# Attention queries and keys loaded straight into TensorE's operand tiles, without staging and casts, with some assumed delays longer

## The chip, the cores and the metric

The kernel runs on one core of one Trainium2 chip. The metric is the device time of one execution, in microseconds (us). The numbers below come from three timed runs and from one profiled execution of the kernel before.

## The reference

One transformer block over 1024 tokens with a model width of 1024, all in float32. A normalised input `h` is projected to four mixers and to 4 x 1024 gates; the mixers' outputs are multiplied by the gates, added, projected by `w_out`, and a convolutional feed-forward part follows.

```
proj = rms_norm(x, g) @ w_in            # s5, sgu, deltanet, attention q k v, 4 x 1024 gates
merged = sum(sigmoid(gate_b) * (mixer_b(...) @ w_br[b]) for b in range(4))
x = x + merged @ w_out
x = x + conv_ffn(rms_norm(x), ...);  return rms_norm(x)

# the attention mixer (diff_attention): 4 heads, each with two maps of 32 channels
s = q . k / sqrt(32) - slope[h] * (qpos - kpos), causal
p = softmax(s);  pd = p[map 0] - lam * p[map 1]
o = rms_norm(pd @ v) * (1 - lam_init)
```

## The kernel before

Matrix products are made to float32 accuracy from float32r operands: a tile is split into a rounded high part (`hi`) and the rest (`lo`), and each product is three matmuls (hi hi, lo hi, hi lo). The kernel's work after the first normalisation is in these stages: the mixers (deltanet, s5, attention projections, sgu), the attention itself (`diff`), the gates that are left, the merge of the four branches, `w_out`, and the feed-forward part.

**The order of the work** is written by `weave` (line 110). It holds a few generators, the *tasks*, and one more, the *filler* (`gates`: 30 blocks of gate columns, 48 matmuls of 512 columns each). A task that has issued what it can yields a number: the delay in us that its author assumes until its next matmuls will have their inputs, most of them from the table `LAT` (line 1733). `weave` counts the matmul time that it has emitted (`pe.now`), and a task whose delay has not passed yet is left alone: another task is taken, and if none is ready a piece of filler. A delay that is too short puts a matmul on TensorE's in-order queue before its inputs are there, and TensorE stands; a longer one puts more of the other tasks' matmuls or of filler in between. What is left of the filler when the tasks are done is run at once, before the merge. Each engine takes its instructions in the order in which they were placed on it.

There are two weaves that matter. In the first, one task is the deltanet (`dn_pair` for two pairs of heads) and then `diff_begin`, which prepares the attention; the other is `z_in`, `s5`, `diff_in` and `sgu`. In the second, the only task is `diff`.

**The attention's operands.** `diff_in` (line 865) projects queries, keys and values of two blocks of 128 channels (`b` = 0, 1: heads 0 and 1, heads 2 and 3) and stores them to DRAM from SP's queue: for each of q and k a tensor of three stacked parts (q: hi, hi, lo; k: hi, lo, hi), so that one matmul over 96 rows makes all three products. `diff_begin` (line 901) computes a few constants, turns the values to tokens (`diff_v`, line 988: a load of 512 KB from SP's queue into a staging tile `stg`, a delay `LAT["dv"]`, transposes on TensorE) and calls `diff_prep`. `diff_prep` (line 958) makes eight operand tiles `stkq0..3`, `stkk0..3` of 105 rows x 1024: it loads 96 rows of q or k and 9 rows of position terms ("alibi") into one of three `stg` tiles, with two DMAs from GpSimd's queue (POOL in the profile), and ScalarE (ACT) casts the staging tile to the operand tile in float32r (line 969). `diff` (line 929) runs the heads 0 to 3; after head 0 it calls `diff_prep` for `b` = 1, whose tiles take the same space as those of `b` = 0, so a cast waits until the head that used that tile is done. `diff_norm` also uses two `stg` tiles.

**Other places the change touches.** `dn_pair` puts 6 transposes on TensorE, yields `LAT["row"]` and then issues a matmul on `rowl` (line 612), which VectorE (DVE) makes at line 609. `s5_groups` (8 times) transposes two tables, yields 0 at line 1212 and then issues a matmul on `NA` (line 1216), a table that DVE finishes at line 1195. After the last group `s5` yields `LAT["s5z"]` (line 1298), loads `z` back from DRAM, splits it into `zh` and `zl` and multiplies.

POOL also makes the `lo` parts of the filler's weights (`glo`, line 152) and of q and k (`ql`), and one product of sgu (`ws`, line 808), which needs the load `tri`.

Of the kernel before, what the change touches and what calls it, by code (L numbers as in the profile page):

```python
# [11 lines left out]
F32 = mybir.dt.float32  # L12
F32R = mybir.dt.float32r
# [8 lines left out]
P = 128  # L22
L = 1024
# [72 lines left out]
class Builder:  # L96
# [438 lines left out]
    def dn_pair(self, pool, pr, src):  # L535

        nc = self.nc
        v = nc.vector
        sq, sk, sv = src
# [46 lines left out]
        rows = []  # L586
# [17 lines left out]
        wq = self.t(pool, [P, 8, 256], F32, "WQ")  # L604
        kq = self.t(pool, [P, 8, 2, 128], F32, "KQ")
        gl = self.t(pool, [P, 16], F32, "gl")
        yield LAT["row"]
        r = self.t(pool, [32, 8, 2], F32R, "rowl")
        v.tensor_tensor(r, pt2[0:32, 128:256].rearrange("p (c t) -> p c t", t=64)[:, :, 63].unsqueeze(1).to_broadcast([32, 8, 2]),
                        delta.unsqueeze(2).to_broadcast([32, 8, 2]), op=ALU.mult)  # L610
# [114 lines left out]
        for ch in range(16):  # L725
            yield LAT["state"] if ch else LAT["wT"]
            m, hf = ch // 2, ch % 2
            rows, other = slice(64 * hf, 64 * hf + 64), slice(64 - 64 * hf, 128 - 64 * hf)
            u = rk_tile[rows, m, 0].rearrange("p h d -> p (h d)")
            p1 = self.ps()  # L730
# [4 lines left out]
            p2 = self.ps()  # L735
# [25 lines left out]
        y = self.t(pool, [P, L], F32, "row", 2)  # L761
        for f in range(2):
            s = slice(512 * f, 512 * f + 512)
# [101 lines left out]
    def diff_in(self):  # L865

        nc = self.nc
        self.qkdram = {}
        self.vdram = []
        with ExitStack() as st:  # L870
            pool = self.pool(st, "dqk", side="right")
            for w, blk in (("q", B_DQ), ("k", B_DK), ("v", B_DV), ("v", B_DV + 1), ("q", B_DQ + 1), ("k", B_DK + 1)):
                b = blk % 2
                if w == "v":
                    d = self.t(self.dp, [P, L], F32, f"dv{b}")
                    self.vdram.append(d)
                else:
                    d = self.t(self.dp, [3, P, L], F32, f"dq{w}{b}")
                    self.qkdram[w, b] = d

                f = self.t(pool, [P, L], F32, "qf", 1)
                if w != "v":
                    hi, lo = self.t(pool, [P, L], F32R, "qh", 1), self.t(pool, [P, L], F32R, "ql", 1)

                def evac(s, ps):
                    if w == "q":
                        nc.scalar.activation(f[:, s], ps, AF.Copy, scale=32.0 ** -0.5)
                    else:
                        nc.scalar.copy(f[:, s], ps)
                    if w != "v":  # L890
                        self.split(hi[:, s], lo[:, s], f[:, s], nc.scalar, nc.gpsimd)

                yield from self.project(blk, evac)
                if w == "v":
                    nc.sync.dma_start(d, f)
                    continue
                for i, x in enumerate((hi, hi, lo) if w == "q" else (hi, lo, hi)):
                    nc.sync.dma_start(d[i], x.bitcast(F32))
        self.projected = True

    def diff_begin(self, stack):

        nc, v = self.nc, self.nc.vector
        while not self.projected:
            yield 1.0
        pool = self.operands = self.pool(stack, "operands", side="left")

        lq = self.t(pool, [P, 2, 2, 32], F32, "lq")
        nc.sync.dma_start(lq, self.a["diff_l"])
        lp = self.t(pool, [P, 2, 32], F32, "lp")  # L910
        ls = self.t(pool, [P, 2], F32, "ls")
        v.tensor_tensor(lp, lq[:, 0], lq[:, 1], op=ALU.mult)
        v.tensor_reduce(ls, lp, axis=AX.X, op=ALU.add)
        le = self.exp_small(pool, ls, [P, 2], "le")
        nlam = self.t(pool, [P, 1], F32, "nlam")
        v.tensor_tensor(nlam, le[:, 1:2], le[:, 0:1], op=ALU.subtract)
        v.tensor_scalar(nlam, nlam, -LAM_INIT, None, op0=ALU.add)
        idb = self.t(pool, [P, 128], BF16, "idb")
        cmb = self.t(pool, [P, 128], BF16, "cmb")
        v.tensor_copy(idb, self.ident)  # L920
        v.tensor_copy(cmb, self.c[:, C_CAUSAL:C_CAUSAL + 128])
        self.diff_consts = nlam, idb, cmb

        self.vhl = self.t(pool, [P, 8, 4, 128], F32R, "vhl")
        for x in range(2):
            yield from self.diff_v(pool, self.vhl, x)
        self.stk = [self.diff_prep(pool, 0)]

    def diff(self, pool):
        nc = self.nc  # L930
        v = nc.vector
        stk, vh = self.stk, self.vhl
        nlam, idb, cmb = self.diff_consts

        held = None
        for h in range(4):
            b, hl = divmod(h, 2)
            for i in range(8):
                if h or i:
                    yield max(0.0, free - self.pe.now)  # L940
                p0 = self.diff_scores(pool, i, stk[b], hl, nlam, idb, cmb)
                done = self.pe.now + LAT["p"] + LAT["p1"] * (i + 1)
                if held:
                    yield max(0.0, held[-1] - self.pe.now)
                    yield from self.diff_values(pool, vh, *held[:-1])
                if i == 0 and hl == 0:
                    if b:
                        yield from self.diff_norm(pool, 0, ob)
                    ob = self.t(pool, [P, L], F32, "ob", 1)
                free = self.pe.now if i < 3 else done - LAT["p2"]  # L950
                held = h, i, p0, ob, done
            if h == 0:
                stk.append(self.diff_prep(self.operands, 1))
        yield max(0.0, held[-1] - self.pe.now)
        yield from self.diff_values(pool, vh, *held[:-1])
        yield from self.diff_norm(pool, 1, ob)

    def diff_prep(self, pool, b):

        nc = self.nc  # L960
        v = nc.vector
        stk = {}
        for hl, w in itertools.product(range(2), "qk"):
            for hm in range(2 * hl, 2 * hl + 2):
                s = self.t(pool, [105, L], F32R, f"stk{w}{hm}", 1)
                g = self.t(pool, [P, L], F32, "stg", 3)[0:105]
                nc.gpsimd.dma_start(g[0:96, :], self.qkdram[w, b][:, 32 * hm:32 * hm + 32, :])
                nc.gpsimd.dma_start(g[96:105, :], self.a["alibi_q"][2 * b + hm // 2] if w == "q" else self.a["alibi_k"])
                nc.scalar.copy(s, g)
                stk[w, hm] = s  # L970
        return stk

    def diff_norm(self, pool, b, ob):
        nc = self.nc
        v = nc.vector
        y = self.t(self.operands, [P, L], F32, "stg", 3)
        sq = self.t(self.operands, [P, L], F32, "stg", 3)
        nc.scalar.activation(sq, ob, AF.Square)
        yield LAT["sq"]
        r = self.rms_scale(pool, sq, self.c[:, C_BLK64:C_BLK64 + 128:64], 1.0 / 64)  # L980
        yield LAT["rsqrt"]
        for f, r in enumerate(self.rms_rows(r, 2)):
            s = slice(512 * f, 512 * f + 512)
            v.tensor_tensor(y[:, s], ob[:, s], r, op=ALU.mult)
            v.tensor_scalar(y[:, s], y[:, s], self.col("diff_norm_g"), 1.0 - LAM_INIT, op0=ALU.mult, op1=ALU.mult)
        nc.sync.dma_start(self.ydram[3][:, b, :], y)

    def diff_v(self, pool, vh, b):

        vf = self.t(pool, [P, L], F32, "stg", 3)  # L990
        self.nc.sync.dma_start(vf, self.vdram[b])
        yield LAT["dv"]
        for f in range(2):
            pt = self.to_tokens(vf, f).rearrange("p (m h d) -> p m h d", m=4, h=2)
            sl = slice(4 * f, 4 * f + 4)
            hi = vh[:, sl, 2 * b:2 * b + 2, 0:64]
            self.nc.scalar.copy(hi, pt)
            self.nc.vector.tensor_tensor(vh[:, sl, 2 * b:2 * b + 2, 64:128], pt, hi.bitcast(F32), op=ALU.subtract)
# [176 lines left out]
    def s5_groups(self, pool, g0, NG, udram, zdram):  # L1175
        nc = self.nc
        v, g_ = nc.vector, nc.gpsimd
        p = self.s5p
# [26 lines left out]
        for W, tag, sc in ((W1, "sF", 1.0), (W2, "sG", -1.0)):  # L1205
# [3 lines left out]
            x = self.t(pool, [P, NG, 128], F32, tag)  # L1209
            nc.scalar.mul(x.rearrange("p g c -> p (g c)"), pt[:, 0:128 * NG], sc)  # L1210
            wt.append(x)
        yield 0.0

        pk = self.ps()
        for g in range(NG):
# [32 lines left out]
        for x, tab, dst in ((wt[0], CT, z), (wt[1], ST, z2)):  # L1248
            pv = self.ps()
# [4 lines left out]
        f = "p g c -> p (g c)"  # L1254
# [12 lines left out]
        y = self.t(pool, [P, NG, 128], F32, "zin")  # L1267
# [462 lines left out]


W_BUFS = {"w": 3, "g": 4, "raw": 2}
LAT = {'dng': 14.76, 'tok': 2.33, 'tok2': 0.31, 'rows': 11.3, 'row': 1.76, 'decay': 0.47, 'gram': 2.75, 'gram2': 0.05, 'subst': 40.0, 'inverse': 10.0, 'solve': 2.1, 'wT': 1.2, 'state': 0.72, 'u': 1.17, 'out': 10.15, 'gelu': 0.93, 'vt': 0.8, 'mix': 0.52, 's5p': 49.2, 's5': 4.25, 's5z': 6.6, 's5v': 1.98, 's5y': 8.2, 'glu': 2.84, 'dv': 8.0, 'p': 1.16, 'p1': 0.14, 'p2': 1.2, 'pv': 2.4, 'sq': 6.1, 'rsqrt': 3.2}
COLS = {}


# [68 lines left out]
```

## Time and profile before

| what | value |
|---|---|
| three runs: median (lowest to highest) | 1773.92 us (1773.41 to 1776.66) |
| the profiled execution: own time, span of its instructions | 1779.1 us, 1777.3 us |
| TensorE (PE): busy, share of the span | 1679.2 us, 94% |
| VectorE (DVE) | 1167.5 us, 66% |
| ScalarE (ACT) | 684.8 us, 39% |
| GpSimd (POOL) | 578.1 us, 33% |
| mean granted TensorE clock | 0.975 of full speed |

Times in the profile are counted from the span's start, in us. An engine's idle time before an instruction is put down to what came last among the things that it waited for; PE's idle time is the difference of the span and 1679.2 us, about 98 us. A name such as `stg<-dqq` is a tile written from a tile or tensor read; `L969` is the line of the kernel.

### The profile page before, as it was taken

Reading aid. Unit: us, or ns where it says so; the run is one execution under the profiler, and the core shown is the slowest. Engines: PE = TensorE matmul, PEld = TensorE weight load, DVE = VectorE, ACT = ScalarE, POOL = GpSimd, SP = SyncE. Lnnn points to the kernel's source line nnn. Section 1 sums busy time; section 2 is a strip of 40 time slices with the busy share of each in tenths; the row PEclk is TensorE's granted clock in tenths of the full one; section 3 lists DMA queues with packets and bytes.
Section 4 is the critical chain, followed back from the end, with each engine's and each line's share of the span. In section 5 each row is a group of like instructions: output and inputs, shape, how many; then the busy total and the mean of one; then the engine's idle time right before and its main releaser. Section 6 shows DMA issues by size and latency. Waiting matters only on the chain.

```text
span 1777.3 us, 22177 instructions
## 1 busy us (share of the span) xinstructions
PE 1679.2 (94%) x7802; PEld 1346.2 (76%) x7802; DVE 1167.5 (66%) x2151; ACT 684.8 (39%) x1204; POOL 578.1 (33%) x473
## 2 busy tenths in 40 slices
PE   7899999999899698999998899999999999999996
PEld 5676877857677576778886687888888888788885
DVE  8895956888334357694068667887787787565342
ACT  4432322221332346563212354444544544354231
POOL 2312223435211221112216443666666663000000
PEclk9899999999999799999999999999999999999998
DMA  4212322213433532114476242222222223674341
GB/s 150 69 60 59 106 73 67 93 61 84 128 130 119 132 110 77 58 60 149 177 247 213 90 142 78 78 77 90 83 77 89 83 78 119 233 247 143 106 131 48
DMA packets 121295, 196.13 MB, mean 110 GB/s; under 512 B 40400, under 2 KB 48336, under 8 KB 120672
## 3 DMA queue, kind: packets, MB, share of 16 engines
q1 hardware_dynamic: 91632, 127.66, 23.2%
q10 hardware_dynamic: 20592, 60.14, 9.4%
q0 software_dynamic: 8960, 6.91, 1.5%
q8 instruction: 62, 1.02, 0.2%
q14 instruction: 49, 0.40, 0.1%
HBM read 141.62 MB, written 52.43 MB: 109 GB/s over the span
## 4 chain that ended last, share of the span: by engine, by line
PE 66%; DVE 14%; DMA 7%; issue 7%; POOL 3%; ACT 1%; SPq 1%; POOLq 0%; ACTq 0%; DVEq 0%
PE qb L89 17%; PE qa L89 14%; PE pd L89 13%; PE pg L89 12%; PE ps L89 8%; DMA stg<-in_alibi_k_dram 2%; DVE acc L1365 1%; PE ps L93 1%; DVE gld L1364 1%; PE p L89 1%; DMA x<-x2d 1%; DVE osb L675 1%; DVE row L676 1%; DMA tri<-in_tri_dram 1%; DVE x L408 1%
## 5 line engine op out<-in xcount | busy, mean ns | idle before, releaser
L89 PE MATMUL pg<-hhi,ghi 128*128 128x512 f32 x496 | 208.5, 420 | 0.0
L152 POOL TENSOR_TENSOR glo<-raw,ghi 128x512 fp32r<-128x512 f32 x72 | 100.4, 1396 | 324.8 <-ACT ghi L145 319.2
L89 PE MATMUL pg<-hhi,glo 128*128 128x512 f32 x496 | 201.7, 407 | 0.0
L89 PE MATMUL pg<-hlo,ghi 128*128 128x512 f32 x496 | 201.2, 406 | 0.0
L145 ACT CAST ghi<-raw 128x512 fp32r<-128x512 f32 x110 | 68.1, 620 | 174.3 <-DVE cv L1600 59.6
L89 PE MATMUL pd<-hhi,whi 128*128 128x512 f32 x312 | 128.6, 413 | 0.0
L89 PE MATMUL pd<-hhi,wlo 128*128 128x512 f32 x312 | 123.0, 394 | 0.2
L89 PE MATMUL pd<-hlo,whi 128*128 128x512 f32 x312 | 123.2, 395 | 0.0
L89 PEld LDWEIGHTS pg<-hhi,ghi 128*128 128x128 f32 x496 | 96.5, 194 | 24.4 <-issue 6.5
L89 PEld LDWEIGHTS pg<-hlo,ghi 128*128 128x128 f32 x496 | 96.7, 195 | 19.3
L89 PEld LDWEIGHTS pg<-hhi,glo 128*128 128x128 f32 x496 | 96.5, 195 | 15.9 <-issue 0.2
L89 PE MATMUL qb<-xh,whi 128*128 128x512 f32 x264 | 103.1, 391 | 1.2 <-ACT whi L145 0.8
L89 PE MATMUL qa<-xh,ghi 128*128 128x512 f32 x264 | 102.8, 390 | 1.1 <-DVE qa L1558 1.1
L89 PE MATMUL qa<-xh,glo 128*128 128x512 f32 x264 | 102.8, 390 | 0.0
L89 PE MATMUL qa<-xl,ghi 128*128 128x512 f32 x264 | 102.8, 389 | 0.0
L89 PE MATMUL qb<-xl,whi 128*128 128x512 f32 x264 | 102.8, 389 | 0.0
L89 PE MATMUL qb<-xh,wlo 128*128 128x512 f32 x264 | 102.7, 389 | 0.0
L1678 POOL TENSOR_TENSOR x<-x,rs 128x512 f32<-128x512 f32 x6 | 7.6, 1286 | 269.3 <-DMA fr<-in_w_down_dram 205.9
L1337 ACT ACTIVATE gate<-pg 128x512 f32<-128x512 f32 x62 | 37.2, 600 | 117.5 <-PE pg L89 117.1
L145 ACT CAST whi<-raw 128x512 fp32r<-128x512 f32 x86 | 53.5, 622 | 62.9 <-PE pd L89 44.4
L89 PEld LDWEIGHTS pd<-hhi,whi 128*128 128x128 f32 x312 | 59.0, 189 | 18.3 <-issue 4.7
L152 POOL TENSOR_TENSOR wlo<-fs,whi 128x512 fp32r<-128x512 f32 x42 | 59.1, 1406 | 42.5 <-ACT whi L145 42.5
(690 smaller groups left out, 4469.4 us busy)
## 6 DMA issues: line engine op xcount, KB each, us to landing
raw<-in_w_in_dram SPq DMA_DIRECT2D x104, 256.0 KB
gates<-gate ACTq DMA_DIRECT2D x32, 512.0 KB
gld<-gates ACTq DMA_DIRECT2D x32, 512.0 KB
fr<-in_w_up_dram SPq DMA_DIRECT2D x44, 256.0 KB
raw<-in_w_up_dram SPq DMA_DIRECT2D x44, 256.0 KB
gd<-cv ACTq DMA_DIRECT2D x22, 512.0 KB
fr<-in_w_dn_dram SPq DMA_DIRECT2D x22, 256.0 KB
fr<-gd SPq DMA_DIRECT2D x22, 256.0 KB
```

The source lines that it names most:

```text
L89: return self.nc.tensor.matmul(out, w, x, **kw)
L93: return self.nc.tensor.transpose(out, x, ident)
L145: eng.copy(out, in_)
L152: (e_lo or self.nc.vector).tensor_tensor(lo, src, hi.bitcast(F32), op=ALU.subtract)
L408: nc.vector.scalar_tensor_tensor(x[:, k, :], x[:, k, :], g[:, k:k + 1], self.rt[:, s], op0=ALU.mult, op1=ALU.mult)
L675: v.tensor_tensor(tv, X[:, 0:m, j].unsqueeze(2).to_broadcast(sh), Ls[:, j, j + 1:32].unsqueeze(1).to_broadcast(sh), op=ALU.mult)
L676: v.tensor_tensor(X[:, 0:m, j + 1:32], X[:, 0:m, j + 1:32], tv, op=ALU.subtract)
L1337: self.nc.scalar.activation(self.gt[i][:, s], ps, AF.Tanh, scale=0.5)
L1364: v.scalar_tensor_tensor(g[:, s], g[:, s], 1.0, ps, op0=ALU.add, op1=ALU.mult)
L1365: (v if (b + c) % 2 or b == 3 else nc.gpsimd).tensor_tensor(acc[:, c, s], acc[:, c, s], g[:, s], op=ALU.add)
L1678: g.tensor_tensor(o, o, rs, op=ALU.mult)
```

## The change

- `diff_prep` takes one head (`hl`) at a time. Its DMAs, still from POOL's queue, write the float32r operand tiles themselves; the staging tile and ACT's cast are gone. The DRAM tensor of q and k is declared float32r. Both calls for `b` = 0 stand where the one call stood; for `b` = 1, head 2's operands are prepared after head 0 and head 3's after head 1.
- `diff_v` loads the values from POOL's queue instead of SP's. `stg` has two tiles instead of three.
- Delays: the one before the matmul on `rowl` 1.76 -> 4.8 (`rowl`), the one at line 1212 0 -> 2.2 (`s5t`, eight times), `s5z` 6.6 -> 12.5, `dv` 8 -> 12 (twice).

```diff
@@ dn_pair
-        yield LAT["row"]
+        yield LAT["rowl"]
         r = self.t(pool, [32, 8, 2], F32R, "rowl")
@@ diff_in
-                    d = self.t(self.dp, [3, P, L], F32, f"dq{w}{b}")
+                    d = self.t(self.dp, [3, P, L], F32R, f"dq{w}{b}")
...
-                    nc.sync.dma_start(d[i], x.bitcast(F32))
+                    nc.sync.dma_start(d[i].bitcast(F32), x.bitcast(F32))
@@ diff_begin
-        self.stk = [self.diff_prep(pool, 0)]
+        self.stk = {}, {}
+        for hl in range(2):
+            self.diff_prep(self.stk[0], 0, hl)
@@ diff
-            if h == 0:
-                stk.append(self.diff_prep(self.operands, 1))
+            if h < 2:
+                self.diff_prep(stk[1], 1, h)
@@
-    def diff_prep(self, pool, b):
-
-        nc = self.nc
-        v = nc.vector
-        stk = {}
-        for hl, w in itertools.product(range(2), "qk"):
-            for hm in range(2 * hl, 2 * hl + 2):
-                s = self.t(pool, [105, L], F32R, f"stk{w}{hm}", 1)
-                g = self.t(pool, [P, L], F32, "stg", 3)[0:105]
-                nc.gpsimd.dma_start(g[0:96, :], self.qkdram[w, b][:, 32 * hm:32 * hm + 32, :])
-                nc.gpsimd.dma_start(g[96:105, :], self.a["alibi_q"][2 * b + hm // 2] if w == "q" else self.a["alibi_k"])
-                nc.scalar.copy(s, g)
-                stk[w, hm] = s
-        return stk
+    def diff_prep(self, stk, b, hl):
+
+        g = self.nc.gpsimd
+        for w in "qk":
+            for hm in range(2 * hl, 2 * hl + 2):
+                s = stk[w, hm] = self.t(self.operands, [105, L], F32R, f"stk{w}{hm}", 1)
+                g.dma_start(s[0:96, :], self.qkdram[w, b][:, 32 * hm:32 * hm + 32, :])
+                g.dma_start(s[96:105, :], self.a["alibi_q"][2 * b + hl] if w == "q" else self.a["alibi_k"])
@@ diff_norm
-        y = self.t(self.operands, [P, L], F32, "stg", 3)
-        sq = self.t(self.operands, [P, L], F32, "stg", 3)
+        y = self.t(self.operands, [P, L], F32, "stg", 2)
+        sq = self.t(self.operands, [P, L], F32, "stg", 2)
@@ diff_v
-        vf = self.t(pool, [P, L], F32, "stg", 3)
-        self.nc.sync.dma_start(vf, self.vdram[b])
+        vf = self.t(pool, [P, L], F32, "stg", 2)
+        self.nc.gpsimd.dma_start(vf, self.vdram[b])
@@ s5_groups
-        yield 0.0
+        yield LAT["s5t"]
@@ LAT
-'row': 1.76, ... 's5z': 6.6, ... 'dv': 8.0
+'row': 1.76, ... 's5z': 12.5, 's5t': 2.2, 'rowl': 4.8, ... 'dv': 12.0
```

## Rows read from the trace of the kernel before

**Rows 1.** The page's first part, busy us, share of the span and instructions of each engine.

```profile
PE 1679.2 (94%) x7802; PEld 1346.2 (76%) x7802; DVE 1167.5 (66%) x2151; ACT 684.8 (39%) x1204; POOL 578.1 (33%) x473
```

**Rows 2.** PE's waits, 80 to 960 us: in total, times, longest.

```profile
PE ps L89 <- DVE rowl L609: 3.5, 2, 3.0
PE ps L89 <- DVE NA L1195: 4.2, 2, 2.4
PE ps L89 <- ACT zh L145: 6.1, 2, 5.9
...
PE ps L93 <- DVE gv L794: 9.0, 1, 9.0
PE ps L93 <- DVE ob L1067: 8.8, 2, 4.6
PE ps L93 <- DVE leq L247: 7.7, 1, 7.7
```

**Rows 3.** Stretches: length, busy (instructions) of PE, PEld, DVE, ACT, POOL, granted clock, DMA, GB/s.

```profile
344.00:364.00 20.00, 15.17 (x62) 10.86 (x61) 15.12 (x37) 2.62 (x6) 9.50 (x11) 0.83 0.19 63
448.00:459.00 11.00, 5.10 (x17) 3.82 (x16) 0.17 (x1) 1.02 (x2) 1.07 (x3) 0.70 0.64 162
582.00:596.00 14.00, 6.35 (x21) 5.20 (x20) 7.66 (x28) 4.50 (x8) 2.99 (x4) 0.63 0.52 130
610.00:623.00 13.00, 4.00 (x14) 3.11 (x13) 3.35 (x11) 4.19 (x7) 2.10 (x4) 0.61 0.55 123
687.00:698.00 11.00, 6.37 (x23) 4.33 (x22) 5.05 (x13) 4.70 (x11) 3.19 (x4) 0.69 0.49 142
727.00:736.00 9.00, 4.79 (x16) 3.59 (x16) 4.05 (x9) 5.29 (x12) 0.34 (x1) 0.81 0.14 42
```

**Rows 4.** PE in order of time: start us, us, instruction, [idle before <-releaser].

```profile
589.92 1.94 PE L93 MATMUL ps<-consts,stg 128*128 128x128 f32 x8 [7.65 <-DVE leq L247]
...
594.64 0.63 PE L89 MATMUL pd<-hhi,whi 128*128 128x512 f32 x1
595.07 0.63 PE L89 MATMUL pd<-hhi,wlo 128*128 128x512 f32 x1
...
596.52 0.39 PE L89 MATMUL pd<-hhi,whi 128*128 128x512 f32 x1
596.75 0.39 PE L89 MATMUL pd<-hhi,wlo 128*128 128x512 f32 x1
```

**Rows 5.** SP's queue and DVE in order of time, around the load of the values.

```profile
576.37 1.26 SPq L991 DMA_DIRECT2D stg<-dv  x1
...
586.37 0.23 DVE L912 TENSOR_TENSOR lp<-lq 128x64 f32<-128x64 f32 x1 [11.36 <-DMA lq<-in_diff_l_dram]
```

**Rows 6.** POOL in order of time, around the same place.

```profile
575.03 0.87 POOL L967 DMA_DIRECT2D stg<-dqq  x1 [0.41 <-DVE cmb L921]
590.94 1.26 POOL L808 TENSOR_TENSOR ws<-ws,tri 128x512 f32<-128x512 f32 x1 [15.04 <-DMA tri<-in_tri_dram]
```

**Rows 7.** The loads of line 967, issue to landing.

```profile
DMA to landing us min/median/max: 8.7/10.1/15.1
```

**Rows 8.** ACT in order of time, a cast and the tanh behind it.

```profile
616.96 1.05 ACT L969 CAST stkk<-stg 105x1024 fp32r<-105x1024 f32 x1 [7.56 <-DMA stg<-in_alibi_k_dram]
617.91 0.63 ACT L793 ACTIVATE gt<-gt 128x512 f32<-128x512 f32 x1
```

**Rows 9.** ACT's waits, 575 to 740 us: in total, times, longest.

```profile
ACT stkk L969 <- DMA stg<-in_alibi_k_dram: 21.5, 5, 7.6
```

**Rows 10.** A stretch within the attention, columns as in rows 3.

```profile
700.00:725.00 25.00, 24.99 (x138) 19.04 (x138) 23.66 (x48) 19.36 (x45) 2.51 (x3) 1.00 0.15 47
```

**Rows 11.** PE in order of time: the last scores of head 0, the first of head 2.

```profile
683.04 0.66 PE L89 MATMUL p<-stkk,stkq 105*128 105x512 f32 x2
...
725.77 0.22 PE L89 MATMUL p<-stkk,stkq 105*128 105x128 f32 x1
```

**Rows 12.** The chain that ended last, in order of time, around the end of the attention.

```profile
827.71 64.16 PE pg L89 x282
```

More of the change, by code (lines that the diff above doesn't have):

```diff
@@ L1732 @@
 W_BUFS = {"w": 3, "g": 4, "raw": 2}
-LAT = {'dng': 14.76, 'tok': 2.33, 'tok2': 0.31, 'rows': 11.3, 'row': 1.76, 'decay': 0.47, 'gram': 2.75, 'gram2': 0.05, 'subst': 40.0, 'inverse': 10.0, 'solve': 2.1, 'wT': 1.2, 'state': 0.72, 'u': 1.17, 'out': 10.15, 'gelu': 0.93, 'vt': 0.8, 'mix': 0.52, 's5p': 49.2, 's5': 4.25, 's5z': 6.6, 's5v': 1.98, 's5y': 8.2, 'glu': 2.84, 'dv': 8.0, 'p': 1.16, 'p1': 0.14, 'p2': 1.2, 'pv': 2.4, 'sq': 6.1, 'rsqrt': 3.2}
+LAT = {'dng': 14.76, 'tok': 2.33, 'tok2': 0.31, 'rows': 11.3, 'row': 1.76, 'decay': 0.47, 'gram': 2.75, 'gram2': 0.05, 'subst': 40.0, 'inverse': 10.0, 'solve': 2.1, 'wT': 1.2, 'state': 0.72, 'u': 1.17, 'out': 10.15, 'gelu': 0.93, 'vt': 0.8, 'mix': 0.52, 's5p': 49.2, 's5': 4.25, 's5z': 12.5, 's5t': 2.2, 'rowl': 4.8, 's5v': 1.98, 's5y': 8.2, 'glu': 2.84, 'dv': 12.0, 'p': 1.16, 'p1': 0.14, 'p2': 1.2, 'pv': 2.4, 'sq': 6.1, 'rsqrt': 3.2}
 COLS = {}
```

## The prediction

> **What bounds the kernel now.** I began with the page's busy times: TensorE works for 94% of the span and no other engine for more than 66% [rows 1]. So the time is that of PE's work, which the change leaves alone matmul for matmul, and of PE's pauses, some 98 us. The next view is the list of PE's waits. The reader is to see that six of its lines, all in the two weaves, hold 39.3 us: 3.5 for `rowl`, 4.2 for `NA`, 6.1 for `zh`, 9.0 for `gv`, 8.8 for `ob`, 7.7 under the name of `leq` [rows 2]. The last name misleads. The instruction that waited is the transposes of `stg`, that is of the values just loaded [rows 4]; the constants that `leq` belongs to were late because their load was, and both loads stood on SP's queue after the stores of q and k [rows 5]. So that wait is for a DMA.
>
> Each pause costs more than itself. In the stretches around them the granted clock is 0.61 to 0.83, a mixture of its two levels, 2.4 and 1.2 GHz [rows 3]. After the pause of 7.65 us PE starts again at 589.92, and its matmuls of 512 columns start 0.43 us apart until 595.5, then 0.23 us apart [rows 4]: 5.6 us of work at the lower level, half of it lost.
>
> After the attention PE runs 282 matmuls of filler without a break for 64.16 us [rows 12]. This is the reserve from which a longer delay is filled, and it shows that a pause taken out earlier brings the merge and all that follows forward by its length: nothing else is waited for at that point.
>
> **The change part by part.** The lost work at the lower clock first, since all parts share it. The low level held for 2 x (1 - clock) x length in each stretch: 6.8, 6.6, 10.4, 10.1, 6.8 and 3.4 us, 44.1 in sum [rows 3]. Measured at one place, 5.6 of 10.4 us of it was work [rows 4]; with that share the six stretches hold 23.8 us of slow work, of which half, 12 us, is lost. At stake are 39.3 + 12 = 51 us.
>
> *Longer delays at `rowl`, `NA` and `zh`.* They add no instruction: other matmuls that PE has to do anyway stand in the gap. `rowl`: 3.04 us more against waits of at most 3.0; nothing left. `NA`: 2.2 more against at most 2.4; 0.2 left. `zh`: 5.9 more against 5.9 [rows 2]; its `zl` part comes from POOL a little later, so I leave 0.5. All lengthened delays together, 2 x 3.04 + 8 x 2.2 + 5.9 + 2 x 4 = 37.6 us, take at most that much from the reserve of 64 us, so the cover holds; if it were gone, PE would stand instead, as now.
>
> *The casts.* ACT loses 16 casts of 1.05 us. What counts is that they hold its queue. At 616.96 a cast that had kept ACT idle for 7.56 us until its DMA landed stood in front of the tanh that makes `gv` [rows 8]. Without it the tanh can come 7.56 + 1.05 = 8.6 us sooner, so of the 9.0 us 0.4 are left; late next is DVE's product. The two `ob` waits are of the same kind: ACT waited 21.5 us for such loads, and DVE's `ob` and the softmax stand behind [rows 9]. I leave 0.5 of 8.8.
>
> *The loads of q and k.* As many DMAs as before on the same queue. In the old order POOL issued one load at 575.03, and the others stood behind the product `ws`, for which POOL waited 15 us [rows 6], and then behind free staging tiles. One cast still waited for its load at 617 [rows 8], and yet PE's list has no wait for an operand tile before head 0 [rows 2]. Now all sixteen DMAs for `b` = 0 can go once that product is through, without the staging tiles' turns between them, so they stay hidden although PE comes some 20 us sooner. The price if such a cover fails is in the last rival. For `b` = 1 POOL now waits for head 0's (later head 1's) last scores itself. Behind it on its queue stand the `glo` splits of filler weights, for which PE's `pg` matmuls wait; but those scores stand on PE's queue just before the call, and the splits are a block of 48 matmuls, some 11 us, ahead. I cost this at nothing, and at a wait of `rowl`'s size, 3 us, at worst.
>
> *The load of the values.* It moves from SP's queue, where it stood behind the stores of q and k, to POOL's, at 575, in the place of the load that was issued there [rows 6]. PE asks for it at 582.3 before; with 4 us more delay at 586.3. Its arrival is bounded by the loads on that queue, 8.7 to 15.1 us [rows 7]: 583.7 to 590.1, so PE waits between nothing and 3.8 us. The lower end is that of loads in quieter stretches, the upper one that of the load issued at this very place, but with both value loads in the other queue beside it. I take the middle, 586.9, and leave 1 us.
>
> The Trainium skill, page "DMA: Bandwidth & Descriptors", section "Rules for kernel authors", says that spreading DMAs over the queues of SP, ACT and GpSimd doesn't help bandwidth, since all run on the same 16 DMA engines. By that rule the load would land when it does now, about 590. The trace bears it out in part: the one load from POOL at 575 took the full 15.1 us. The rival of the late values, below, is this case.
>
> *The sum.* Left are 0 + 0.2 + 0.5 + 0.4 + 0.5 + 1 = 2.6, so 36.7 us of waits go, and 11 of the 12 us of slow work (1 kept for the values): 47.7. The new delays also put instructions where none stood before; for that I set one new wait of the kind of `NA` or `rowl`, 2.4 to 3.0 us, with the slow work behind it, 4 us together. It remains a gain of 44 us. The profiled execution took 1779.1 us, so it becomes 1735; the median of the runs is 5.2 us below it, so 1730.
>
> **The rivals.**
> *The values land late.* At 590.1 PE waits 3.8 us instead of 1, and the stretch keeps its slow work, 2.8 us: 6 us less gained, 1736. For it speaks the 15.1 us, against it that 1 MB of value loads and the place behind the stores leave SP's queue.
> *DVE becomes the bound of the attention.* In the stretch 700 to 725 it is busy for 23.66 of 25 us [rows 10]. If heads 0 and 1 can't go faster than DVE, the 8.8 us of `ob` and their slow work, (6.8 + 3.4) x 0.54 / 2 = 2.8, come back in small waits: 1742. Against it: in that same stretch PE works for 24.99 of 25 us.
> *Half the waits come back elsewhere,* because the order that the delays write fits less well at new places: half of 44 is gained, 1752.
> *Slower: loads straight into float32r tiles are slow.* The trace has no load between these types. The place is head 2: its four loads can be issued only after head 0's last scores at 683.7, and its first scores run at 725.8 [rows 11], some 6 us sooner once the longer `ob` wait, 4.6 us [rows 2], and the slow work behind it, 6.8 x 0.54 / 2 = 1.8 us [rows 3], are gone: 36 us for four loads. If they take t each, one after another, PE stands 4t - 36 before head 2 and about as long before head 3. This eats the whole gain from 2 x (4t - 36) = 44 on, t = 14.5 us. With the longest landing, 15.1 us [rows 7], and no overlap, it is 49 us: 1779. Against it: the landing times were taken with up to three loads in flight, so loads on this queue overlap, and the median is 10.1 us.
> The Trainium skill (same page, section "SWDGE vs HWDGE vs iDMA") says that a float32r destination always casts and that only GpSimd's DMAs can do it. It gives no rate for such a cast, and no row here shows one.
>
> **How the numbers follow.** The forecast has 0.60, the late values 0.13, the DVE bound 0.13, half the waits 0.07, slow loads 0.05; 0.02 remain for no effect. The measurement can tell about 0.2%, 3.5 us, from no change. All but the last two lie far below that: faster 0.93, same 0.02, slower 0.05. The low end is the whole 51 us and no new wait, 1722, and a little for my share of slow work: 1720. The high end takes in the rivals up to the half: 1752.
>
> **What would show it.** Right: the six waits of rows 2 gone from PE's list or under 1 us each; granted clock 1.0 in the stretches of rows 3; no instruction of line 969 left; the run of filler after the attention shorter by some 20 to 35 us; the attention's first scores some 35 us sooner. Wrong: a PE wait on an operand tile `stk` before heads 0, 2 or 3; the transposes of `stg` still waiting for more than 4 us; new waits at `p` or `ps` behind DVE; `pg` waiting for `glo`. The likeliest error is in the size of the slow work and in waits that the new order makes.

## The result and the profile after

The changed kernel takes 1754.0 us, the median of four runs (1744.2 to 1757.0), against 1775.3 for the kernel before on the same chip: a ratio of 0.986, 95% interval 0.982 to 0.991. The profiled execution went from 1779.1 to 1755.6 us, its span from 1777.3 to 1753.9. So the gain is 21 us by the medians and 23 by the profiled executions, where 44 were forecast. The time of one kernel varies by some 16 us from run to run here (ten runs of the changed kernel lie between 1744.2 and 1760.3), so below I rest causes on the waits in the traces and on ratios, not on a few microseconds of a median.

The page's busy times of the changed kernel, which answer to [rows 1]:

```profile
PE 1668.4 (95%) x7802; PEld 1337.8 (76%) x7802; DVE 1177.3 (67%) x2151; ACT 668.0 (38%) x1188; POOL 579.2 (33%) x475
```

PE's busy time fell by 10.8 us with the same 7802 matmuls, while the mean granted clock rose from 0.975 to 0.983. Its pauses (span less busy time) fell from 98.1 to 85.5 us, by 12.6, where some 34 us were to go. The fall in busy time looks like the forecast (10 to 11), but it isn't that firm: a second profile of the same changed kernel (e9, below) has 1674.7 us busy and pauses of 82.7, so there the falls are 4.5 and 15.4 us. PE's list of waits between 80 and 950 us of the changed kernel shows why; the columns are those of [rows 2]:

```profile
PE pd L89 <- ACT gv L815: 6.0, 1, 6.0
PE ps L93 <- DVE K L1214: 5.6, 1, 5.6
PE pd L89 <- ACT whi L145: 5.5, 2, 5.0
PE pd L89 <- DVE wlo L152: 5.2, 1, 5.2
...
PE ps L89 <- ACT zh L145: 2.3, 2, 2.0
...
PE ps L93 <- DVE ob L1063: 0.2, 1, 0.2
```

The six waits of [rows 2] are gone but for 2.3 us at `zh` and 0.2 at `ob`. In their place stand four lines that the kernel before did not have at this size, 22.3 us together. They have their own stretches at the lower clock, here in the view by stretches (columns as in [rows 3]):

```profile
184.00:194.00 10.00, 8.13 (x29) 6.61 (x30) 9.96 (x40) 3.67 (x6) 2.00 (x2) 0.83 0.22 69
362.00:372.00 10.00, 6.78 (x22) 5.39 (x23) 8.54 (x20) 0.60 (x1) 2.63 (x5) 0.66 0.13 35
600.00:614.00 14.00, 9.95 (x48) 7.96 (x46) 0.00 (x0) 0.67 (x2) 3.08 (x6) 0.94 0.87 85
614.00:632.00 18.00, 11.06 (x32) 8.16 (x33) 12.55 (x34) 6.62 (x12) 2.94 (x4) 0.67 0.47 114
```

By the prediction's formula, 2 x (1 - clock) x length, the low level held there for 3.4 + 6.8 + 1.7 + 11.9 = 23.8 us; with its share of 0.54 of work, half of it lost, that is 6.4 us. So the new places cost 22.3 + 6.4 = 28.7 us, where the prediction had set 4.

The prediction's own marker in time says where the gain is missing. PE reaches the attention's first scores only 9.9 us sooner (before, then after):

```profile
655.89 0.22 PE L89 MATMUL p<-stkk,stkq 105*128 105x128 f32 x1
645.97 0.22 PE L89 MATMUL p<-stkk,stkq 105*128 105x128 f32 x1
```

From there to the run of filler behind the attention (827.71 [rows 12], now 805.38) it takes 159.4 us instead of 171.8, 12.4 less. The prediction's share for the attention was 8.3 for `ob` and 2.8 of slow work, 11.1. So that part came in full, and what is missing is missing in the first weave.

**The two waits near 620 us.** The chain that ended last runs through one load of weights, and ACT, in order of time, shows how it reaches PE:

```profile
591.33 21.92 DMA raw<-in_w_in_dram
```

```profile
613.33 0.62 ACT L145 CAST ghi<-raw 128x512 fp32r<-128x512 f32 x1 [17.79 <-DMA raw<-in_w_in_dram]
613.85 0.58 ACT L834 COPY vt<-ps 128x512 f32<-128x512 f32 x1
614.33 1.07 ACT L993 CAST vhl<-ps 128x512 fp32r<-128x512 f32 x2
615.28 0.61 ACT L815 COPY gv<-pd 128x512 f32<-128x512 f32 x1
```

Weights of 256 KB take 21.9 us to land. The cast of them that stands at the head of ACT's queue keeps it for 17.8 us; `vt`, `vhl` and the copy that frees the psum of `gv` stand behind it, and PE waits for that copy (6.0 us). The wait for `whi` follows from the same stop: DVE had stood for `vt` and works off from 614.5 us what was held up, a tanh on ACT waits 7.7 us for one of these products, and the cast of `whi` stands behind the tanh, at 624.75. A staging cast that held ACT's queue has been taken out, and a filler's cast now holds it. While the weights are on their way, the view of DMA queues shows, 589 to 603 us (packets, MB, share of 16 engines):

```profile
q0 software_dynamic: 231, 0.95, 91.8%
q1 hardware_dynamic: 89, 0.17, 12.0%
```

GpSimd's queue (q0), which carries the direct loads, fills the engines to 92% and moves 0.95 MB in 14 us, 68 GB/s; the weights' queue (q1) moves 0.17 MB. Each 4 KB of q0 costs 0.918 x 16 x 14 us / (0.95 MB / 4096 B) = 0.89 us of engine time. The four loads of head 0 are on their way here; they landed 28 to 30 us after their issue. POOL issued the ninth of the loads of q, k and alibi only when the first had landed:

```profile
609.24 0.68 POOL L966 DMA_DIRECT2D stkq<-dqq  x1 [22.34 <-DMA stkq<-dqq]
```

The loads of head 1, which convert as well, are these later ones. They were on their way four at a time too, and the same view for 613 to 622 us has:

```profile
q0 software_dynamic: 1573, 1.36, 70.7%
```

That is 151 GB/s and, by the same working, 0.31 us for each 4 KB; they landed in 9 to 12 us. So a group of four converting loads isn't slow wherever it runs.

**The two waits near 186 and 365 us** have nothing to do with loads. At 365 PE waits for `K`, and `K` stands behind one multiplication on DVE that waits for a product of POOL, which stands behind four others and a filler's split:

```profile
363.37 1.47 DVE L1190 TENSOR_TENSOR s5tt<-s5pi,s5bc 128x256 f32<-128x256 f32 x1 [4.84 <-POOL sB L1236]
364.76 0.41 DVE L1214 COPY K<-ps 16x256 f32<-16x256 f32 x1
```

```profile
357.68 0.73 POOL L1233 TENSOR_TENSOR sA<-sA,s5tt 128x256 f32<-128x256 f32 x1
358.37 1.92 POOL L582 TENSOR_TENSOR RK<-RK,sc 128x1024 f32<-128x1024 f32 x1
...
361.40 1.25 POOL L152 TENSOR_TENSOR glo<-raw,ghi 128x512 fp32r<-128x512 f32 x1
362.62 0.71 POOL L1236 TENSOR_TENSOR sB<-sB,s5tt 128x256 f32<-128x256 f32 x1
```

At 186 the split `wlo` stands on DVE behind a run of instructions, most of them small S5 products. ACT's cast of `whi` ran at 175.30; from 176 to 186 us DVE is busy all the time with 65 instructions, and the split comes near the end of them (columns as in [rows 3], then DVE):

```profile
176.00:186.00 10.00, 4.84 (x22) 3.70 (x20) 10.00 (x65) 0.63 (x1) 1.86 (x4) 0.98 0.00 0
```

```profile
185.13 0.68 DVE L152 TENSOR_TENSOR wlo<-raw,whi 128x512 fp32r<-128x512 f32 x1
```

### The profile page after: what moved, and what is told of

It reads as the page before. It is cut to its first block, busy times and chain, and to the rows that moved or that the text cites. A ratio compares the mean times of both kernels' runs of the same rounds, so it can differ in the third digit from the quotient of the medians.

```text
span 1753.9 us, 22139 instructions
## 1 busy us (share of the span) xinstructions
PE 1668.4 (95%) x7802; PEld 1337.8 (76%) x7802; DVE 1177.3 (67%) x2151; ACT 668.0 (38%) x1188; POOL 579.2 (33%) x475
## 4 chain that ended last, share of the span: by engine, by line
PE 72%; DVE 13%; issue 6%; DMA 5%; POOL 2%; ACT 2%; SPq 1%; POOLq 0%; DVEq 0%; ACTq 0%
PE qb L89 18%; PE pd L89 17%; PE qa L89 14%; PE pg L89 14%; PE ps L89 7%; DMA raw<-in_w_in_dram 2%; PE ps L93 1%; DVE acc L1361 1%; PE p L89 1%; DVE gld L1360 1%; DVE x L408 1%; DVE row L676 1%; DMA fr<-gd 1%; DMA fr<-in_w_dn_dram 1%; DVE osb L675 1%
## 5 line engine op out<-in xcount | busy, mean ns | idle before, releaser
L89 PE MATMUL pd<-hhi,whi 128*128 128x512 f32 x312 | 130.3, 418 | 12.5 <-ACT gv L815 6.0
L89 PEld LDWEIGHTS pd<-hhi,wlo 128*128 128x128 f32 x312 | 59.9, 192 | 16.9 <-DVE wlo L152 6.6
```

Source lines behind the costliest of these rows:

```text
L89: return self.nc.tensor.matmul(out, w, x, **kw)
```

## The experiments

Three theories went into them. The converting loads hold the DMA engines (T1), or their number at one time does (T2), and that makes the waits near 620 us. The longer delays give another order in the first weave (T3), and that makes those near 186 and 365 us.

**The delays alone** (e1).

```diff
 (the kernel before)
-        yield LAT["row"]
+        yield LAT["rowl"]
...
-        yield 0.0
+        yield LAT["s5t"]
...
-LAT = {..., 's5z': 6.6, ..., 'dv': 8.0, ...}
+LAT = {..., 's5z': 12.5, 's5t': 2.2, 'rowl': 4.8, ..., 'dv': 12.0, ...}
```

> The kernel before with the four delays of the change alone (rowl, s5t, s5z, dv); staging, casts and queues as before. Theory (the new order of the first weave brings waits of its own): rowl, NA and zh lose their 13.8 us of waits, but the two new waits of the changed kernel, 5.2 us for wlo near 186 us and 5.6 us for K near 365 us, stand here too, with stretches at the lower clock behind them; about 4 us of gain remain, some 1771 us, and the waits for gv, ob and the values are as before. Rival (the longer delays are worth what was forecast, the new waits come from the loads): 13.8 us of waits and some 3.6 us of slow work go, 1758 us, and neither new wait is in PE's list.

Measured: 1772.0 us, ratio 0.9972 (0.9960 to 0.9985). PE's waits:

```profile
PE ps L93 <- DVE ob L1067: 9.4, 3, 5.7
PE ps L93 <- DVE K L1218: 5.6, 1, 5.6
PE pd L89 <- DVE wlo L152: 5.5, 1, 5.5
PE pd L89 <- ACT whi L145: 4.8, 2, 4.2
...
PE ps L93 <- DVE gv L794: 3.6, 1, 3.6
PE pd L89 <- ACT gv L815: 3.1, 1, 3.1
```

T3 holds: `K` and `wlo` are there without a single direct load, and the delays alone are worth 0.3%. Two more things stand in this trace. PE waits 10.9 us between 596 and 630 us, for `gv` twice and for `whi`, the last two because ACT stands for the loads of staging casts (7.3 us before 616.9, 6.1 before 627.1): a wait at this place needs no direct load, only something late at the head of ACT's queue. And the wait under the name of `leq` is gone, though the values are still loaded from SP's queue.

**The direct loads alone** (e2): the changed kernel with `'rowl': 1.76, 's5t': 0.0, 's5z': 6.6, 'dv': 8.0`.

> The changed kernel with the four delays of the kernel before: direct loads on GpSimd's queue, values too, but rowl 1.76, s5t 0, s5z 6.6, dv 8. Theory: the waits near 186 and 365 us are gone and rowl, NA and zh are back, which is nearly a draw, so 1754 to 1760 us, with the waits at gv and whi near 615 to 625 us as in the changed kernel. Rival: the delays carry most of the gain, 1771 us.

Measured: 1756.8 us, ratio 0.9874 (0.9857 to 0.9892). `K` and `wlo` are gone from PE's list, `zh`, `rowl` and `NA` are back, and there is one for `gv`:

```profile
PE pd L89 <- ACT gv L815: 8.7, 1, 8.7
PE ps L89 <- ACT zh L145: 5.2, 2, 5.0
PE ps L89 <- DVE rowl L609: 5.1, 2, 4.6
PE ps L89 <- DVE NA L1191: 4.2, 2, 2.4
```

So the loads carry the gain; on top of them the delays add nothing that these intervals can tell. The wait for `gv` comes again from ACT standing for weights of the filler, 9.5 and 8.6 us, though these loads landed in 12.5 and 7.7 us. So that wait doesn't need the slow landing of the changed kernel either.

**Head 1's loads later** (e3).

```diff
-        for hl in range(2):
-            self.diff_prep(self.stk[0], 0, hl)
+        self.diff_prep(self.stk[0], 0, 0)
...
+        self.diff_prep(self.stk[0], 0, 1)
         held = None
```

> The changed kernel, but the direct loads of head 1 are issued at the start of the attention instead of together with those of head 0: four converting loads in flight near 580 to 610 us instead of eight. Theory (the eight converting loads together keep the DMA engines from the weights that the filler needs): the 256 KB of weights issued near 591 us land in 10 to 14 us instead of 21.9, the waits for gv and whi (6.0 and 5.5 us) shrink to under 2 us each, the stretches at the lower clock behind them go, about 12 us less: 1742 us. Rival (the weights are late for another reason, or the wait is ACT's order): the waits stay, 1754 us. A cost that it may bring: head 1's loads are late and PE waits for stk between heads 0 and 1.

Measured: 1750.3 us, ratio 0.9833 (0.9818 to 0.9848). The load of weights on the chain, and q0 from 593 to 603 us:

```profile
596.42 13.01 DMA raw<-in_w_in_dram
```

```profile
q0 software_dynamic: 324, 1.15, 90.4%
```

The weights land in 13 us, `gv`'s wait is gone from PE's list, `whi` keeps 3.2 us. But the reason isn't the one that T2 gives: POOL issued head 1's loads from 605 us on all the same, as soon as an earlier load had landed, and in the changed kernel too it issued them only at 609 us, for the same reason. Both kernels had head 0's four loads in flight at that time, and here these moved at 115 GB/s instead of 68 (0.52 us for each 4 KB). What the edit did change is when they start: the first is issued at 586.2 us, in the changed kernel at 581.0.

**Staged float32 loads, paced** (e4): each tile is loaded as float32 into one of three staging tiles, 5 us apart, and cast on ACT two to three loads later.

```diff
+        for hl, w, m in itertools.product(range(2), "qk", range(2)):
+            self.diff_load(0, hl, w, m)
+            yield 5.0
+            if len(self.raw) == 3:
+                self.diff_cast()
```

> The changed kernel with staging back in another form: the operands are loaded as float32 without conversion into three staging tiles, one load every 5 us from 580 us on, and each is cast on ACT two to three loads later, when it has landed, so that ACT's queue doesn't stand for a DMA. The second pair of heads is loaded and cast inside heads 1 and 2 in the same way. Theory (the price of the change lies in the converting loads): landing of the loads 9 to 12 us, weights near 591 us in under 14 us, waits for gv and whi gone, no wait for ob, 1740 us. Rival (the conversion is not what costs, the order is): waits of 5 to 6 us at gv and whi remain or come elsewhere, 1754 us or more; ACT's 16 casts of 1.05 us come back, and if one still stands for its load the old wait for ob, 4 us each, comes back as well.

Measured: 1766.0 us, ratio 0.9932 (0.9917 to 0.9947). Neither theory's number. The weights were in time (ACT waited 4.4 us for them), but ACT's queue stood for its own loads again, inside the heads, and PE behind it:

```profile
757.88 1.04 ACT L983 CAST stkq<-stg 105x1024 fp32r<-105x1024 f32 x1 [6.52 <-DMA stg<-in_alibi_q_dram]
```

```profile
PE ps L89 <- ACT pth L1066: 6.0, 1, 6.0
...
PE ps L89 <- DVE ptl L1067: 3.8, 1, 3.8
```

This is the old `ob` wait under other names: of what the direct loads are worth, a good part is that ACT's queue is rid of the casts.

**Further loads by themselves** (e5), which nothing reads, written into the last two heads:

```diff
+        if (h, i) == (2, 3):
+            f = self.t(self.operands, [P, L], F32, "stg", 2)
+            g.dma_start(f[0:96, :], src[:, 0:32, :].bitcast(F32))
+        if (h, i) == (2, 5):
+            r = self.t(self.operands, [P, L], F32R, "prb", 1)
+            g.dma_start(r[0:96, :], src[:, 32:64, :])
...
```

> The changed kernel with eleven further loads of 384 KB (96 rows of 4 KB of the stored queries) in the last two heads of the attention, where the DMA engines are mostly idle; nothing reads them. In head 2 one as float32 and one with conversion from GpSimd's queue and one as float32 from SP's; in head 3 four as float32 at once, and later four with conversion at once. Theory (converting loads cost the DMA engines much more): at least half as long again for the converting one alone, and for the four together about twice the time of the four float32 ones. Rival (the conversion costs nothing, the crowd near 590 us was the cause): equal within 1 us alone and within 3 us for four.

One run, 1759.4 us. The single loads from GpSimd's queue landed in 9.1 us (float32, at 722.7) and 9.2 us (converting; it depends on nothing, so it was issued at 618.9 already, while three of head 1's converting loads were on their way). So a converting load of 384 KB isn't slower as such, not even beside three others, and T1 in its simple form falls. The loads by fours never came together: POOL stood between them for the tiles, and they landed in 9.7 to 12.2 us, both kinds mixed.

**The same loads without conversion** (e6).

```diff
-                s = stk[w, hm] = self.t(self.operands, [105, L], F32R, f"stk{w}{hm}", 1)
-                g.dma_start(s[0:96, :], self.qkdram[w, b][:, 32 * hm:32 * hm + 32, :])
+                s = self.t(self.operands, [105, L], F32, f"stk{w}{hm}", 1)
+                g.dma_start(s[0:96, :], self.qkdram[w, b][:, 32 * hm:32 * hm + 32, :].bitcast(F32))
...
+                stk[w, hm] = self.one
```

> The changed kernel with the same loads at the same places and from the same queue, but into float32 tiles, so without conversion; nothing reads these, and the scores of all heads read one tile that is filled with a constant, so the computation of the scores is left out in favour of scores of equal numbers, instruction for instruction as before. Theory (the conversion keeps the DMA engines busy): the weights issued near 591 us land in under 12 us, the waits for gv and whi (11.5 us) go, and with the slow work behind them 15 us: 1739 us, as far below the version in which head 1 is loaded later (1750) as that is below the changed kernel. Rival (it is the number of loads at once): the weights still take about 20 us and the waits stay, 1754 us.

Measured: 1751.8 us, ratio 0.9865 (0.9845 to 0.9886). On the chain, and q0 from 593 to 601 us:

```profile
595.31 11.96 DMA raw<-in_w_in_dram
```

```profile
q0 software_dynamic: 332, 1.15, 70.3%
```

Nothing reads the loaded tiles here; the scores of all heads are left out in favour of scores of a constant tile. The same four loads move at 144 GB/s, 0.32 us for each 4 KB, and the weights land in 12 us instead of 22. `gv` is gone from PE's list, `whi` has 2.1 us. T2 falls with it: the changed kernel, e3 and this one have the same four loads of q and k in flight at that time, so their number can't make the difference. That the conversion alone makes it isn't shown either: the first load starts at 586.1 us here, 5 us later than in the changed kernel and as in e3, where the weights landed in 13 us with conversion. (With no reader the tiles of `b` = 1 were free at once, so all sixteen tiles were loaded before the attention, but the other twelve came later.) The time still fell hardly at all: with the second half of the loads on their way the store of `gv` took 8.5 us, DVE's first `dmx` of the attention stood 8.9 us for it, and PE waited 4.9 us behind that at 647.8. One wait went, and another came at a transfer further on.

**Which delay makes the new order** (e7, e8): one delay goes back in each.

```diff
 (e7)
-LAT = {..., 's5t': 2.2, ...}
+LAT = {..., 's5t': 0.0, ...}
 (e8)
-LAT = {..., 'rowl': 4.8, ...}
+LAT = {..., 'rowl': 1.76, ...}
```

> The changed kernel with the delay before the first S5 products back at 0 (s5t 2.2 to 0), all else kept. Theory (the 2.2 us let other work of DVE and GpSimd in ahead, and that makes the wait of 5.6 us for K near 365 us): K goes, NA comes back with 4.2 us, about 3 us less with the slow work, 1751 us; the wait of 5.2 us for wlo near 186 us stays. Rival (the wait for K comes from rowl's delay, which shifts the order from the start): K stays at 5.6 us and NA is back on top of it, 1759 us.

Measured: 1753.7 us, ratio 0.9877 (0.9860 to 0.9894). `K` went, but `wlo` stayed (6.2 us), and new ones of 2.7 to 4.6 us came at `p`, `row` and `zin` (two). A swap.

> The changed kernel with the delay at rowl back from 4.8 to 1.76, all else kept. Theory (this delay alone moves the S5 parameters ahead of the filler's splits on DVE and makes the wait of 5.2 us for wlo near 186 us): wlo goes, and rowl comes back with 3.5 to 5 us and the wait for KQ with 2.5: 1754 to 1757 us. Rival: wlo stays and rowl is back as well, 1761 us.

Measured: 1747.7 us, ratio 0.9843 (0.9823 to 0.9862).

```profile
PE ps L89 <- DMA KQ<-dnX: 9.1, 2, 6.6
PE pd L89 <- ACT gv L815: 7.2, 1, 7.2
...
PE ps L89 <- DVE rowl L609: 2.5, 2, 2.0
...
PE pd L89 <- DVE wlo L152: 0.2, 1, 0.2
```

It is `rowl`'s delay that makes `wlo` late: without it `wlo` is gone, as in e2. `K` goes with either delay (e7, e8), so its wait needs both. `gv`'s wait is there for another reason than in the changed kernel. ACT's copy waited for a store, not for weights:

```profile
599.14 0.58 ACT L815 COPY gv<-pd 128x512 f32<-128x512 f32 x1 [10.81 <-DMA dqk<-qh]
```

The order has moved the first direct loads ahead of the last stores of q and k (issued at 588 to 590 us), and ACT waits for one of these now.

**The changed kernel again** (e9), timed beside the last three.

> The changed kernel once more, unaltered, as the reference for the versions timed beside it: 1752 to 1756 us, ratio to the kernel before 0.986 to 0.988.

Measured: 1755.0 us, ratio 0.9865 (0.9841 to 0.9889). The weights took 20.28 us, `gv`, `whi`, `wlo` and `K` cost 4.4, 5.3, 5.2 and 5.6 us: the waits repeat.

**Converting loads, paced** (e10).

```diff
+                self.diff_prep(self.stk[0], 0, hl, w, m, True)
+                yield 6.0
...
+        if gate:
+            self.nc.vector.memset(s[0:32, 0:1].bitcast(F32), 0.0)
         g.dma_start(s[0:96, :], self.qkdram[w, b][:, 32 * hm:32 * hm + 32, :])
```

> The changed kernel, its converting loads kept, but for the first two heads written out one tile every 6 us, each held until a one-element write of DVE into the tile has run, so that they don't start together. Theory (a converting load is cheap by itself and dear only among others): the 4 KB packets of GpSimd's queue take under 300 ns at the median in 580 to 625 us (886 in the changed kernel at 595 to 601 us), the weights issued near 591 us land in under 12 us, the waits for gv and whi fall from 11.5 to under 4 us, 1742 to 1748 us. Rival (each converting load costs the engines the same wherever it runs): packets stay at 500 ns and more, and the weights are as late as before, 1754 us.

Measured: 1753.0 us, ratio 0.9855 (0.9827 to 0.9883). Nothing follows from it: DVE ran all eight small writes between 583.5 and 584.4 us, since they too depend on nothing, so the loads went as before. The weights took 19.1 us.

**The better versions together** (e11 has the edits of e3 and e8, e12 those of e10 and e8).

> The changed kernel with head 1's loads issued at the start of the attention and rowl's delay back at 1.76: the two versions that gained 4 and 6 us alone. If the two causes (the crowd of loads near 590 us, the order of the first weave) are apart, the gains add up: 1743 us. If the order that the delays write decides everything, the mixture is as likely to lose as to gain, 1748 us or more, with the waits for KQ (9 us) and one near gv still there.

> The paced converting loads together with rowl's delay back at 1.76. If the causes are apart: the waits for wlo, K, gv and whi are all gone, KQ and rowl (11 us) are back, 1740 us. Rival (the order decides): gv's wait of 7 us stays as with rowl's old delay alone, 1748 us.

Measured: 1752.1 us, ratio 0.9854 (0.9838 to 0.9869), and 1756.5, 0.9872 (0.9855 to 0.9890). The gains don't add up: both have `KQ` with 9.3 us and `gv` with 7.2 and 7.4, as e8 has, and e12 has a new wait of 5.5 us at `gate`. That the order decides fits this. The fastest ratios were those of e3 and e8; their intervals just overlap that of e9, so I don't call either better.

## Why the prediction came out as it did

The median, 1754.0 us, lies 2 us beyond the high end of the range, 1752; with the kernel before at 1775.3 instead of 1773.9, the ratio of 0.986 answers to 1750 us, just inside. Either way it is the edge of the range, where the prediction had put "half the waits come back". The mechanism was right for the waits that it named; the gain was half of the forecast.

*What was to go, went.* 2.6 us of the six waits were to be left, 2.5 are. `zh` kept 2.3 instead of 0.5, the values cost nothing instead of 1. A wait of 2.5 us for the load of `KQ`, which stands in the whole list of the kernel before but not in the rows shown, went as well; I had not counted it. Waits of 39.3 - 2.5 = 36.8, all 12 us of slow work, since the values kept none, and `KQ` make 51.3 us.

*The step that failed is the last term of the sum*, "one new wait of the kind of `NA` or `rowl`", 4 us. It measured 28.7 us, four waits with the slow work behind them. 51.3 - 28.7 = 22.6, and the span fell by 23.4. That the two agree so well is partly luck: by this account waits fall by 17.0 and slow work by 5.6, and the page has 12.6 less of pauses and 10.8 less of busy time. PE's other waits, none above 3.7 us in total, rose from 9.1 to 14.5 us in the same lists, which the account leaves out, and the busy time differs by 6 us between two profiles of the changed kernel. Three statements stand behind that term:
- "They add no instruction: other matmuls that PE has to do anyway stand in the gap." True of the gap, but the matmuls that fill it bring their DVE and POOL work along. Moved ahead, it made `wlo` and `K` late (e1, e2, e7, e8). Of 17 us forecast for the delays, 5 came (e1: 0.3%).
- "Now all sixteen DMAs for `b` = 0 can go once that product is through." Only eight could: POOL stood 22.3 us at the ninth.
- "so they stay hidden", of the loads of q and k. They are, for their own readers: PE has no wait of note for `stk` before any head. The price fell on others that use the engines at the time: the filler's weights, through the queue of ACT (e3 and e6, where the weights land in 13 and 12 us and `gv`'s wait is gone), elsewhere a store (e6, e8). I had asked only who waits for the loads, not what waits beside them.

*The rivals.* "Half the waits come back elsewhere" (1752, a chance of 0.07) is what happened, though part of it by the loads. Slow converting loads did come, but at head 0 alone (28 to 30 us) and not at heads 2 and 3: the loads of `b` = 1 landed in 10.4 to 13.8 us with time to spare. The values landed in 4.7 us at the median and PE waited for nothing: the Trainium skill's rule (page "DMA: Bandwidth & Descriptors", section "Rules for kernel authors"), that another queue doesn't help, is about bandwidth, and the trace doesn't agree with the landing of about 590 that I derived from the rule: they landed at 583.4 and 586.1. That leaving the place behind the stores is what did it isn't shown: with the longer delays alone (e1) the load stands on SP's queue, and its wait is gone too. DVE did not become the attention's bound: the attention takes 12.4 us less, head 2's first scores run at 706.87 instead of 725.77 [rows 11], and `ob` has 0.2 us left.

*The signs.* The attention's first scores came 9.9 us sooner instead of 35. Of the six stretches of [rows 3], four have a granted clock of 1.00 now, the first has 0.98, and 610 to 623 us, where the new waits stand, has 0.72. POOL's waits for head 0's and 1's scores (13.8 us in four) reached no matmul, as costed. The run of filler after the attention was to shrink by 20 to 35 us and didn't; it answers to [rows 12]:

```profile
805.38 65.52 PE pg L89 x288
```

It begins 22.3 us sooner and is as long. The longer delays took nothing from this reserve: 288 matmuls were left in it, 282 before.

*Open.* Each 4 KB on q0 cost 0.89 us of engine time in the changed kernel and 0.52 in e3 while head 0's four loads were on their way, 0.31 with head 1's four in the changed kernel, all with conversion, and 0.32 with head 0's four without it (e6). So neither the conversion nor four loads at a time is enough to make a load dear. What else it takes at 589 to 603 us no run here tells; when the loads start differed between these runs (581.0 us in the changed kernel, 586 in e3 and e6) and was not varied by itself, and a version with one converting load in flight at a time was not reached.

## What to carry to other kernels

When a transfer is called hidden, ask not only who reads it but what else needs the DMA engines, and which engine's queue stands for that. A longer delay in a written order is not free where it is filled: the filling work brings work for other engines, so look at who is late behind that before counting the wait as won. Of several such edits, time each alone: here one of two carried the gain, and two variants that each looked a little faster did not add up.

## What the runs showed of the hardware

- One float32 to float32r load of 384 KB landed as fast as a plain one (9.2 us beside three other converting loads, 9.1 with none beside it; e5). Four in flight held the engines at 92% for 68 GB/s at 589 to 603 us of the changed kernel, and four others at 71% for 151 GB/s at 613 to 622 us of the same execution; four plain ones took 70% for 144 GB/s (e6).
- GpSimd stood at a DMA issue for 22.3 us, with eight loads of q, k and alibi out, until the first of them had landed. In the trace that issue waits for the semaphore that the first load signals, so the wait stands in the program. The filler's split behind it on its queue, whose weights landed at 613.3, ran at 615.67.
- Two profiles of the same changed kernel have PE busy for 1668.4 and 1674.7 us with the same 7802 matmuls.
- The start of the kernel alone (0 to 80 us) had a granted clock between 0.87 and 0.96 in these profiles, with no change there.
